# A trunk layer's output projection: from a plain product to a block product of seven, with the last branch computed in tile pairs

## The chip, the cores and the metric

The kernel runs on one core of a Trainium2 chip. Its engines work side by side, each through its own queue in order: TensorE (PE in the profile; the loading of its stationary operand is listed as PEld), VectorE (DVE), ScalarE (ACT), GpSimd (POOL) and SyncE (SP), which here only issues transfers. GpSimd issues transfers as well, those that add to what lies at the destination. The metric is the time of one execution on the device, in microseconds, as the median of several runs.

## The reference

Two layers (`DEPTH` = 2) over 512 tokens of width 1024. A layer projects its input, computes three branches (retention, chunked attention, differential attention), mixes them with sigmoid gates, and sends the mix through one output projection; a residual, a layer norm and a SwiGLU feed-forward part follow. The lines that matter:

```python
g = jax.nn.sigmoid(gates + b_merge[l]).reshape(B, S, N_BRANCHES, D)
merged = (g[:, :, 0] * jnp.einsum('bse,ed->bsd', o_a, w_branch_a[l])
          + g[:, :, 1] * jnp.einsum('bse,ed->bsd', o_b, w_branch_b[l])
          + g[:, :, 2] * jnp.einsum('bse,ed->bsd', o_c, w_branch_c[l]))
mix = jnp.einsum('bsd,de->bse', merged, w_out[l])
x = _layer_norm(DEEPNORM_ALPHA * x + mix, ln1_g[l], ln1_b[l])
```

`mix` is a product of 512 x 1024 with 1024 x 1024.

## The kernel before

**Precision.** Every float32 operand is carried as a pair, a high and a low part of 32 bits (`Pair`, with `hi` and `lo`); a product of two is three matmuls (`mm3`, L121 to L124): high by high, high by low, low by high. ScalarE makes the high part by a cast or an activation (L106 and L108 for activations, L154 and L271 for weights), VectorE the low part by a subtraction (L112, L114, L155, L272).

**Items.** The layer is a list of items, one after the other: an item is a block of weights (its `specs`) and a function that multiplies with it. `run_items` fetches the weights up to three items ahead (`AHEAD` = 3): a transfer into one of four staging tiles `st`, then the split into one of three buffers `wh` and `wl`. An item's split therefore waits until the matmuls of the item three before it are done. Small steps (the `s_...` functions) are handed to an item as groups and run between its halves (`between`). From this written order a scheduler makes the order of each engine's instructions; that order is fixed when the program is built, and each engine keeps to it on the chip.

**Block products.** The input projections and the feed-forward part already use the seven-product scheme (`Quarters`, `Halves`, `Chain`, `Close`, `Twins`). Activations and weights are cut into 2 x 2 blocks, and instead of eight block products there are seven, called m1, m2, y, x, v, g and h, of sums of blocks. `Quarters` holds the activation side for one pair of tiles k and k + 4 (features) with the two halves of the tokens as the other cut: m1, m2 and h are blocks as they are, `left` makes the sums for y and x (tile s12), `right` those for v and g (s43). For the weight side, `Chain` holds one staging tile: W11 for m1; to it GpSimd adds W12 (for y), then W22 (for x), then W21 (for h), each by a transfer that accumulates (`more`, L178). Such a transfer may begin only when the tile has been split for the product before it. A second tile, loaded ahead with `ahead_c`, holds the weights of g. m2 and v load theirs plainly. `product` computes 128 tokens of a block product in one bank of PSUM, 12 matmuls, twice per product; x, g and h go on accumulating on the banks of m1, and v on that of y, so a later product may not begin on a bank before VectorE has taken the earlier state from it.

**Around the change.** A gate block (`u_gate`, 256 columns) leaves two tiles `th`; those in `EARLY` are stored to DRAM and loaded again when a branch needs them. `u_branch` multiplies the branch by its weights (256 columns, four k-tiles for branch 2), applies the gate (L1080) and adds to the sum (L1084). After branch 2 it splits the sum of all eight tiles into pairs `mg`. The output projection is then three items: `u_out0` twice, for output columns 0 to 511 in four banks, and `u_out1`, columns 512 to 1023, token tile by token tile. `u_out1` adds the residual (`residual`, L1144), takes statistics, and normalises a token tile while PE works on the next (`Norm.normalise`, with one small power on GpSimd); transposes of finished tiles run between, and `to_T` makes the transposed, split input of the feed-forward part. The last of it, for the second half of the tokens, is `s_turned`, run inside the first feed-forward product.

## Time and profile before

| | us |
|---|---|
| median of 3 runs (1879.7 to 1881.35) | 1881.29 |
| the profiled execution | 1878.05 |
| its span, first to last instruction | 1876.3 |
| PE busy, 8802 matmuls | 1861.7 |
| VectorE busy | 1353.3 |
| ScalarE busy | 973.0 |
| GpSimd busy | 120.2 |

Times are from one profiled execution. A row of the timeline gives start, duration, engine, line of the kernel, operation and tiles, and in brackets the idle time before it and what ended that. A group's row gives a count, the busy time and the mean of one in ns. A wait's row says who waited for whom, the sum, how often, and the longest. Matmuls overlap, so what one costs is read from the distance of their starts. In the first layer the output projection runs from 553.6 (the first matmul into `pn`) to about 598.

### The profile page before, as it was taken

How to read it: one execution, taken by the hardware profiler on the slowest of the kernel's cores; microseconds unless marked ns; L12 is line 12 of the kernel's file. 1: busy time of each engine (PE TensorE's matmuls, PEld its weight loads, DVE VectorE, ACT ScalarE, POOL GpSimd, SP SyncE). 2: the span in 40 equal slices, each digit the busy share in tenths (PEclk: the TensorE clock that was granted, in tenths of full speed). 3: DMA queues.
4: the chain of work that ended last, by engine and by line, in shares of the span. 5: the costliest groups of instructions: out<-in, count | busy, mean ns of one | idle time of the engine just before them, and what ended most of it. 6: DMA issues, size and time to landing. Idle time of an engine off the chain costs nothing. (4 is left out here: it accounts for less than half of the span.)

```text
span 1876.3 us, 23317 instructions
## 1 busy us (share of the span) xinstructions
PE 1861.7 (99%) x8802; PEld 1553.8 (83%) x8802; DVE 1353.3 (72%) x2059; ACT 973.0 (52%) x1579; POOL 120.2 (6%) x145
## 2 busy tenths in 40 slices
PE   9999999999999999999999999999999999999998
PEld 7788888888888888888878888888888888888886
DVE  6777766667766776888686777566776667778886
ACT  5545555567643445554364546545666344455541
POOL 2000000000000000010020000000000001000100
PEclk9999999999999999999999999999999999999999
DMA  9585344332146577787386844533321547777871
GB/s 295 164 267 155 123 139 132 102 124 90 57 144 171 157 191 191 192 224 198 127 232 192 252 112 127 170 112 109 124 68 57 189 125 178 196 197 201 200 194 45
DMA packets 220320, 296.59 MB, mean 158 GB/s; under 512 B 8500, under 2 KB 115088, under 8 KB 220208
## 3 DMA queue, kind: packets, MB, share of 16 engines
q1 hardware_dynamic: 194096, 244.35, 39.3%
q0 software_dynamic: 26112, 50.76, 15.5%
q8 instruction: 69, 1.13, 0.2%
q14 instruction: 43, 0.35, 0.1%
HBM read 271.95 MB, written 23.12 MB: 157 GB/s over the span
## 5 line engine op out<-in xcount | busy, mean ns | idle before, releaser
L122 PE MATMUL pt<-xTh,wh 128*128 128x512 f32 x960 | 377.1, 393 | 2.1 <-ACT wh L154 2.0
L272 DVE TENSOR_TENSOR wl<-st,wh 128x2048 fp32r<-128x2048 f32 x126 | 288.1, 2289 | 119.3 <-ACT wh L271 118.7
L124 PE MATMUL pt<-xTh,wl 128*128 128x512 f32 x960 | 374.1, 390 | 0.0
L123 PE MATMUL pt<-xTl,wh 128*128 128x512 f32 x960 | 373.8, 389 | 0.0
L271 ACT CAST wh<-st 128x2048 fp32r<-128x2048 f32 x126 | 240.6, 1912 | 206.8 <-PE pf L124 107.8
L155 DVE TENSOR_TENSOR wl<-st,wh 128x1024 fp32r<-128x1024 f32 (+1 forms) x204 | 219.2, 1094 | 63.2 <-ACT wh L154 57.1
L154 ACT CAST wh<-st 128x1024 fp32r<-128x1024 f32 (+1 forms) x204 | 188.7, 949 | 115.4 <-PE pt L123 36.4
L122 PEld LDWEIGHTS pt<-xTh,wh 128*128 128x128 f32 x960 | 180.3, 188 | 39.3 <-ACT wh L154 2.9
L124 PEld LDWEIGHTS pt<-xTh,wl 128*128 128x128 f32 x960 | 180.2, 188 | 38.0
L123 PEld LDWEIGHTS pt<-xTl,wh 128*128 128x128 f32 x960 | 180.4, 188 | 36.2 <-DVE xTl L112 0.2
L122 PE MATMUL pf<-wh,xTh 128*128 128x512 f32 x336 | 132.6, 395 | 1.4 <-ACT rph L106 0.8
L123 PE MATMUL pf<-wl,xTh 128*128 128x512 f32 x336 | 131.1, 390 | 0.0
L124 PE MATMUL pf<-wh,xTl 128*128 128x512 f32 x336 | 131.0, 390 | 0.0
L746 ACT COPY tc<-pf 128x512 f32<-128x512 f32 x84 | 48.4, 588 | 80.5 <-PE pf L124 76.1
L122 PE MATMUL pf<-wh,s12h 128*128 128x512 f32 x224 | 88.0, 393 | 0.0
L122 PE MATMUL pf<-wh,s43h 128*128 128x512 f32 x224 | 87.3, 390 | 0.0
L123 PE MATMUL pf<-wl,s12h 128*128 128x512 f32 x224 | 87.3, 390 | 0.0
L124 PE MATMUL pf<-wh,s12l 128*128 128x512 f32 x224 | 87.2, 390 | 0.0
L123 PE MATMUL pf<-wl,s43h 128*128 128x512 f32 x224 | 87.2, 389 | 0.0
L124 PE MATMUL pf<-wh,s43l 128*128 128x512 f32 x224 | 87.2, 389 | 0.0
L122 PEld LDWEIGHTS pf<-wh,xTh 128*128 128x128 f32 x336 | 63.1, 188 | 16.5 <-ACT rph L106 1.6
L124 PEld LDWEIGHTS pf<-wh,xTl 128*128 128x128 f32 x336 | 63.0, 188 | 13.5 <-DVE xTl L112 0.4
(318 smaller groups left out, 3707.7 us busy)
## 6 DMA issues: line engine op xcount, KB each, us to landing
st<-in_w_in SPq DMA_DIRECT2D x61, 1024.0 KB, 5.1
st<-in_w_ffn_in SPq DMA_DIRECT2D x38, 1024.0 KB, 5.6
st<-in_w_ffn_in POOLq DMA_DIRECT2D x20, 1024.0 KB, 11.3
st<-in_w_ffn_out SPq DMA_DIRECT2D x20, 1024.0 KB, 7.8
st<-in_w_in SPq DMA_DIRECT2D x32, 512.0 KB, 5.0
st<-in_w_ffn_out POOLq DMA_DIRECT2D x16, 1024.0 KB, 9.2
st<-in_w_in POOLq DMA_DIRECT2D x12, 1024.0 KB, 10.6
th<-th SPq DMA_DIRECT2D x48, 256.0 KB, 4.3
```

What stands on the lines that cost most here:

```text
L122: nc.tensor.matmul(ps, lh, rh, start=start, stop=False, skip_group_check=onto)
L123: nc.tensor.matmul(ps, lh, rl, start=False, stop=False, skip_group_check=onto)
L124: nc.tensor.matmul(ps, ll, rh, start=False, stop=stop, skip_group_check=onto)
L154: return [nc.scalar.copy(self.hi[:, a:b], self.st[:, a:b]), nc.vector.tensor_sub(self.lo[:, a:b], self.st[:, a:b], f(self.hi[:, a:b]))]
L155: nc.vector.tensor_sub(self.lo[:, a:b], self.st[:, a:b], f(self.hi[:, a:b]))]
L271: nc.scalar.copy(self.hi, st)
L272: nc.vector.tensor_sub(self.lo, st, f(self.hi))
L746: nc.scalar.copy(t[to, j], ps)
```

## The change

The output projection becomes seven products of 24 matmuls (four k-tiles, two times 128 tokens, three matmuls each), with a `Chain` over `w_out`. `out_items` writes them in the order m1, m2, y, x, v, g, h; `plus` (now for both users) adds each product to the residual tiles z. The token tiles 0 and 1 are normalised after v, the tiles 2 and 3 after h; the transposes of the first half stand behind g, those of the second inside the first feed-forward product.

So that a pair of tiles is ready together, gate and branch blocks of branch 2 now compute the tiles i and i + 4 instead of 2i and 2i + 1, from two loads of 128 columns. The sum of the first is split at once for m1, that of the second for m2 and h; `left` and `right` follow as steps. Gate block 1 of branch 2 is no longer in `EARLY` and moves from before the differential attention to behind it; gate block 3 moves between the second and third block of branch 2. Some steps of the attention branches move to a neighbouring item.

```diff
-EARLY = [(0, 0), (0, 1), (0, 2), (0, 3), (2, 0), (2, 1)]
+EARLY = [(0, 0), (0, 1), (0, 2), (0, 3), (2, 0)]
...
+        def tiles(br, i):
+            return (i, i + 4) if br == 2 else (2 * i, 2 * i + 1)
+
+        def cols_of(w, c, br, i):
+            return [w[:, c + P * d:c + P * d + P] for d in tiles(br, i)] if br == 2 else [w[:, c + 256 * i:c + 256 * i + 256]]
...
-                    if br == 2:
-                        mg[d] = Pair("mg")
-                        split(mg[d], acc.pop(d), scale=0.5)
+                    if br == 2 and j == 0:
+                        q = mq[d] = Quarters()
+                        pr = HalfPair("m1")
+                        split(pr, acc[d][:, q.A], scale=0.5)
+                        q.put("m1", pr, q.A)
+                    elif br == 2:
+                        pr = Pair("m2")
+                        split(pr, acc[d], scale=0.5)
+                        mq[d - 4].put("m2", pr, q.A)
+                        mq[d - 4].put("h", pr, q.B)
...
-            (u_gate(1, 3), *d(6)), (u_branch(1, 3), *d(7)), (u_gate(2, 2), [s_d4(2)], [s_d2(3)]),
-            (u_gate(2, 3), [s_d3(3)], [s_d4(3)]),
-            (u_branch(2, 0),), (u_branch(2, 1),), (u_branch(2, 2),), (u_branch(2, 3),),
+            (u_gate(1, 3), *d(6)), (u_branch(1, 3), *d(7)), (u_gate(2, 1), [s_d4(2)], [s_d2(3)]),
+            (u_gate(2, 2), [s_d3(3)], [s_d4(3)]),
+            (u_branch(2, 0), [], [s_mleft(0)]), (u_branch(2, 1), [], [s_mleft(1)]), (u_gate(2, 3), [s_mright(0)], [s_mright(1)]),
+            (u_branch(2, 2), [], [s_mleft(2)]), (u_branch(2, 3), [], [s_mleft(3)]),
...
-        for i in range(2):
-            item(*u_out0(i, banks0))
-        item(rows_of(w_out[l], 512), u_out1)
...
+            hv = Chain(w_out[l], 0, 4)
...
+                    on = {"x": "m1", "g": "m1", "h": "m1", "v": "y"}.get(name, name)
+                    for j in range(2):
+                        t = 2 * i + j
+                        w[on, j] = product(mq, name, j, wt, w.pop((on, j), None))
+                        plus(x1, t, hf, w[on, j], op, last)
+                        if name in ("m2", "v", "h"):
+                            w.pop((on, j))
+                        if whole:
+                            x1["n"].normalise(t)
+                        between()
...
+        for (specs, fn), *groups in [
+            (o["m1"], [s_mright(2)], [o["c"]]), (o["m2"], [s_mright(3)]), (o["y"],), (o["x"],), (o["v"],),
+            (o["g"], [], [s_turned(0)]), (o["h"],),
+        ]:
+            item(specs, fn, *groups)
```

How the built programs stand at the places of the prediction, for the first layer. A number behind a name tells tiles of one name apart; in brackets stands what the instruction waits for (DMASW is a transfer issued by GpSimd, DMAHW one by SyncE).

ScalarE's queue before, at the start of the output projection: the weights of the last branch block and of the projection's items, and between them the high parts of the sums `mgh`.

```order
L154 CAST wh_4999<-st_4998 128x1024 [waits DMAHW6_49,PE_49,Activation_49]
L154 CAST wh_4999<-st_4998 128x1024
L154 CAST wh_5045<-st_5044 128x1024 [waits DMAHW0_49,PE_49,Activation_49]
L154 CAST wh_5045<-st_5044 128x1024
L108 ACTIVATE mgh_4948<-th_2583 128x512 [waits DVE_49]
L108 ACTIVATE mgh_4975<-th_2794 128x512
```

ScalarE's queue now: `wh_5079`, `wh_5150` and `wh_5256` are the weights of y, x and h, all from the chain's staging tile `st_4978`; `wh_5194` and `wh_5226` those of v and g; `m1_5050` is the fourth activation of m1, `s43h_5173` the fourth of v and g.

```order
L271 CAST wh_5079<-st_4978 128x2048 [waits DMASW4_49,PE_49,Activation_49]
L108 ACTIVATE s12h_5025<-sa_5022 128x512 [waits DVE_49]
L108 ACTIVATE m1_5050<-th_2584 128x256 [waits DVE_49]
L108 ACTIVATE m2h_5068<-th_3156 128x512 [waits DVE_49]
L108 ACTIVATE s12h_5075<-sa_5072 128x512 [waits DVE_49]
L271 CAST wh_5150<-st_4978 128x2048 [waits DMASW5_49,PE_49,Activation_49]
L271 CAST wh_5194<-st_5192 128x2048 [waits DMAHW0_49,PE_49,Activation_49]
L271 CAST wh_5226<-st_5147 128x2048 [waits DMASW3_49,PE_49,Activation_49]
L108 ACTIVATE s43h_5129<-sb_5126 128x512 [waits DVE_49]
L271 CAST wh_5256<-st_4978 128x2048 [waits DMASW6_49,PE_49,Activation_49]
L108 ACTIVATE s43h_5173<-sb_5170 128x512 [waits DVE_49]
```

Where the queue held casts of plain loads, three casts now wait for an accumulating transfer, and activations of m1 and of v stand behind them.

PE's queue now, in product v (banks `pf_5198` and `pf_5212`), from its seventh matmul on:

```order
L122 MATMUL pf_5198<-wh_5194,s43h_5129 128x512 [waits Activation_49]
L123 MATMUL pf_5198<-wl_5195,s43h_5129 128x512
L124 MATMUL pf_5198<-wh_5194,s43l_5130 128x512 [waits DVE_49]
L122 MATMUL pf_5212<-wh_5194,s43h_4940 128x512 [waits DVE_49]
L123 MATMUL pf_5212<-wl_5195,s43h_4940 128x512
L124 MATMUL pf_5212<-wh_5194,s43l_4941 128x512
L122 MATMUL pf_5198<-wh_5194,s43h_5173 128x512 [waits Activation_49]
```

PE's queue before, at the start of the projection: `mgh_4877` is the first of the eight sums, and the four banks take it in turn.

```order
L122 MATMUL pn_5088<-wh_4953,mgh_4877 128x512 [waits Activation_49]
L123 MATMUL pn_5088<-wl_4954,mgh_4877 128x512 [waits DVE_49]
L124 MATMUL pn_5088<-wh_4953,mgl_4878 128x512
L122 MATMUL pn_5089<-wh_4953,mgh_4877 128x512
L123 MATMUL pn_5089<-wl_4954,mgh_4877 128x512
```

The old projection multiplies sums that were split during the branch; the new one waits within a product for sums that are made while it runs. The same holds in m1, whose 14th matmul is the first to read `m1_5050`.

VectorE's queue before, between the two halves of the projection's output columns: `z` are the residual tiles, `pn` and `po` the banks.

```order
L1144 SCALAR_TENSOR_TENSOR z_5064<-z_5064,pn_5090 128x512 [waits DMAHW4_49,PE_49]
L1144 SCALAR_TENSOR_TENSOR z_5066<-z_5066,pn_5091 128x512 [waits DMAHW6_49,PE_49]
L478 BN_STATS bn_5086<-z_5064 128x6 [waits DVE_49]
L478 BN_STATS bn_5087<-z_5066 128x6 [waits DVE_49]
L272 TENSOR_TENSOR wl_5199<-st_5196,wh_5198 128x2048 [waits Activation_49]
L1144 SCALAR_TENSOR_TENSOR z_5061<-z_5061,po_5203 128x512 [waits DMAHW1_49,PE_49]
```

VectorE's queue now, from the last low part for v to the first addition of g, which frees a bank for h:

```order
L114 SCALAR_TENSOR_TENSOR s43l_5174<-sb_5170,s43h_5173 128x512 [waits Activation_49]
L1175 SCALAR_TENSOR_TENSOR z_5085<-z_5085,pf_5112 128x512 [waits DMAHW3_49,PE_49]
L1175 SCALAR_TENSOR_TENSOR z_5087<-z_5087,pf_5133 128x512 [waits DMAHW5_49,PE_49]
L272 TENSOR_TENSOR wl_5257<-st_4978,wh_5256 128x2048 [waits DMASW6_49]
L1177 TENSOR_TENSOR z_5085<-z_5085,pf_5198 128x512 [waits DVE_49,PE_49]
L1177 TENSOR_TENSOR z_5087<-z_5087,pf_5212 128x512 [waits DVE_49,PE_49]
L478 BN_STATS bn_5108<-z_5085 128x6 [waits DVE_49]
L478 BN_STATS bn_5109<-z_5087 128x6 [waits DVE_49]
L495 BN_AGGR mv_5274<-bn_5108 128x2 [waits DVE_49]
L272 TENSOR_TENSOR wl_5305<-st_5302,wh_5304 128x2048 [waits Activation_49]
```

Two weight blocks and the additions of x and v now stand between that low part and the addition that h waits for.

More of the change, by code (lines that the diff above doesn't have):

```diff
@@ L289, in put, with left @@
             self.use[name] = pr.hi[:, sl], pr.lo[:, sl]
-        def left(self, t1, t2):
+        def left(self, t1, t2, scale=None):
             a, b = self.A, self.B
@@ L1188, in layer, with plus, out_items, it @@
-        item(rows_of(w_out[l], 512), u_out1)
+                load_rows(x["z"][t], src[P * t:P * t + P])
+        def plus(x, t, hf, ps, op, final=False):
+            z = x["z"][t][hf]
+            if (t, hf) in x["fresh"]:
+                x["fresh"].remove((t, hf))
+                nc.vector.scalar_tensor_tensor(z, z, ALPHA, ps, op0=ALU.mult, op1=op)
+            else:
+                nc.vector.tensor_tensor(z, z, ps, op=op)
+            if final:
+                x["n"].stats(t, hf)
+        def out_items():
+            hv = Chain(w_out[l], 0, 4)
+            w = {}
+            def it(name, i, hf, op, last=False, whole=False):
+                def fn(wt):
+                    if name == "m1":
+                        load_res(x1, x_in if l == 0 else saved[2 * l - 1])
+                        x1["n"] = Norm(x1["z"], v["g1"], v["b1"], bcast_rows(ln1_g[l:l + 1]), bcast_rows(ln1_b[l:l + 1]),
+                                       x1T, saved[2 * l], x1f)
+                    on = {"x": "m1", "g": "m1", "h": "m1", "v": "y"}.get(name, name)
[8 more added lines that the diff above has]
+                        between()
+                return [getattr(hv, name)], fn
+            add, sub = ALU.add, ALU.subtract
+            return {"c": hv.ahead_c, "m1": it("m1", 0, 0, add), "m2": it("m2", 0, 0, add, True), "y": it("y", 1, 1, add),
+                    "x": it("x", 0, 1, sub), "v": it("v", 0, 1, add, True, True), "g": it("g", 1, 1, sub, True),
+                    "h": it("h", 1, 0, add, True, True)}
@@ L1329, in fn @@
                         for i, hf, op in adds:
-                            plus(2 * i + j, hf, w[on, j], op, gi == 1 and name == "h")
+                            plus(x2, 2 * i + j, hf, w[on, j], op, gi == 1 and name == "h")
                         if name in ("m2", "v", "h"):
@@ L1349, in plain @@
                     proj_N(hid, wts, t, ps, REST)
-                    plus(t, 0, ps, ALU.add, t < NT // 2)
+                    plus(x2, t, 0, ps, ALU.add, t < NT // 2)
                     between()
@@ L1359, in chase @@
                         n.transposes(t - 1)
-                    plus(t, 1, ps, ALU.add, True)
+                    plus(x2, t, 1, ps, ALU.add, True)
                     if last:
```

111 lines of the change are left out of this document (38 added, 73 removed).

## The prediction

> **What bounds the kernel now.** First the page: how much of the span TensorE (PE) works. Then the table of waits, for PE alone; then PE's timeline, because "busy" counts matmuls that overlap.
>
> ```profile
> span 1876.3 us, 23317 instructions
> PE 1861.7 (99%) x8802; PEld 1553.8 (83%) x8802; DVE 1353.3 (72%) x2059; ACT 973.0 (52%) x1579; POOL 120.2 (6%) x145
> ...
> core 0: 1876.3 us, clock 0.999
> ...
> PE pt L122 <- ACT wh L154: 2.0, 2, 1.3
> PE warm L583 <- POOL ident masks.py:199: 1.5, 1, 1.5
> PE pf L122 <- ACT rph L106: 0.8, 2, 0.4
> PE px L509 <- DVE z L500: 0.7, 2, 0.4
> ...
> 553.62 0.39 PE L122 MATMUL pn<-wh,mgh 128*128 128x512 f32 x1
> ...
> 555.88 0.39 PE L123 MATMUL pn<-wl,mgh 128*128 128x512 f32 x1
> ```
>
> PE waits for about 5 us in the whole span: every removed matmul is time won, every new wait is time lost. A 128x512 matmul is listed with 0.39 us, but ten start within 555.88 - 553.62 = 2.26 us, so one costs 0.226 us. That corrects the saving by almost half.
>
> **What is removed.** The projection had 8 x 8 x 3 = 192 matmuls in each layer; seven products of 24 are 168. 24 x 0.226 = 5.43 us a layer, 10.85 us in all. A product lasts 5.43 us; in this time whatever the next products need must be made. So the question is which of the new preparations take longer than their cover.
>
> **The chain of weight sums.** One staging tile holds W11 for m1, then by three GpSimd transfers the sums for y, x and h. Each can be issued only when VectorE has read the tile for the product before. The feed-forward part does the same with more work between; there one link is seen whole:
>
> ```profile
> 805.63 2.28 DVE L272 TENSOR_TENSOR wl<-st,wh 128x2048 fp32r<-128x2048 f32 x1
> ...
> 808.21 1.28 POOL L178 DMA_DIRECT2D st<-in_w_ffn_out  x1 [3.48 <-DVE wl L272]
> 824.82 1.28 POOL L178 DMA_DIRECT2D st<-in_w_ffn_out  x1 [15.33 <-DVE wl L272]
> ...
> 820.29 1.91 ACT L271 CAST wh<-st 128x2048 fp32r<-128x2048 f32 x1 [2.37 <-DMA st<-in_w_ffn_out]
> ...
> 822.23 2.29 DVE L272 TENSOR_TENSOR wl<-st,wh 128x2048 fp32r<-128x2048 f32 x1 [0.63 <-ACT wh L271]
> ...
> DMA to landing us min/median/max: 8.1/10.7/14.3
> ...
> DMA to landing us min/median/max: 8.3/10.1/12.0
> ```
>
> VectorE ends y's low half at 807.91, GpSimd issues at 808.21, the data lands 12.0 later (the last row is of the issues at 808.21 and 824.82: 12.0 and 8.3), ScalarE casts from 820.29, the low half is ready at 824.52: 16.6 us for a link. The row above it holds all 48 such transfers. In the new stage y is followed by x at once.
>
> When a link can start is set by the weight buffers: three, so an item's cast waits for the matmuls of the item three before.
>
> ```profile
> 564.74 2.00 ACT L154 CAST wh<-st 128x1024 fp32r<-128x1024 f32 x2 [6.06 <-PE pn L124]
> ...
> 596.40 1.92 ACT L271 CAST wh<-st 128x2048 fp32r<-128x2048 f32 x1 [0.58 <-PE po L124]
> ...
> 598.35 2.29 DVE L272 TENSOR_TENSOR wl<-st,wh 128x2048 fp32r<-128x2048 f32 x1 [1.18 <-ACT wh L271]
> ...
> 593.01 0.56 ACT L534 ACTIVATE xf<-px,colv 128x256 f32<-128x256 f32 x1 [15.47 <-PE px L509]
> 593.61 0.41 ACT L106 CAST xTh<-xf 128x256 fp32r<-128x256 f32 x1
> 593.92 0.56 ACT L534 ACTIVATE xf<-px,colv 128x256 f32<-128x256 f32 x1
> ...
> 574.82 1.28 DVE L478 BATCH_NORM_STATS2 bn<-z 128x6 f32<-128x512 f32 x2
> 576.02 1.27 DVE L1144 SCALAR_TENSOR_TENSOR z<-z,pn 128x512 f32<-128x512 f32 x2
> ...
> 612.99 1.42 DVE L112 TENSOR_TENSOR xTl<-xf,xTh 128x256 fp32r<-128x256 f32 x4
> ```
>
> The first cast began 0.3 us after the 48 matmuls that held its buffer (553.62 + 48 x 0.226 = 564.47). Cast and subtraction of a block take 600.64 - 596.40 = 4.24 us. Two 512-wide VectorE operations start 1.20 apart from the next two: 0.60 each; four 256-wide ones take 1.42: 0.35 each; a low half 2.2 back to back.
>
> Now in order, with 0 at m1's first matmul, in each layer:
> - m1's buffer is that of the last gate block, which ends 48 matmuls earlier, at -10.9. Low half ready at -10.9 + 0.3 + 4.24 = -6.3, the transfer W11+W12 issued at -6.0. Its landing is bounded by 8.1 and 14.3; little else moves then (one 1 MB load), so I take 8.5, by the 8.3 of the issue at 824.82: +2.5.
> - ScalarE's queue has y's cast ahead of the last s12 and of the high half of m1's fourth activation. The cast waits for the landing; then 1.92 + 0.55 + 0.35: 5.3. PE wants that activation with its 14th matmul, at 13 x 0.226 = 2.9. **Wait 2.4.** m1 ends at 5.3 + 11 x 0.226 = 7.8, m2 at 13.2, y at 18.7.
> - Behind s12 (4.95) VectorE has 0.6 + 0.35 + 0.6 and y's low half: 8.8. Issue 9.1. Now the eight loads of z and four of the norm's rows (3 MB) run beside it, so I take the median, 10.7: 19.8; x's low half at 24.0. x needs it with its second matmul at 18.9. **Wait 5.1**; x ends at 24.0 + 23 x 0.226 = 29.2.
> - Issue of h's sum at 24.3; the loads are over, 8.7: 33.0. ScalarE has h's cast ahead of the last s43 high half: 33.0 + 1.92 + 0.6 = 35.5. v wants it with its 13th matmul, at 29.2 + 2.7 = 31.9. **Wait 3.6**; v ends at 38.2, g at 43.6.
> - VectorE, held by that s43, then works off 0.6 + two additions for x 1.2 + h's low half 2.2 + two additions for v 1.2 + two statistics 1.2 + 0.2 + the next item's low half 2.2 + 0.5 + g's addition 0.6 = 9.9: 45.4. h accumulates on the bank that this addition reads. **Wait 1.8.** Two late steps of the normalisation stand right behind.
> - The first feed-forward product starts directly behind the transposes of the first half. A tile costs ScalarE 0.91 (593.01 to 593.92), with two half-block casts of about 1.0 between the first ones, while PE uses a tile in 6 x 0.226 = 1.36. Before, this half was ready a whole token tile earlier. Between 0 and 2.5, I take **1.1**, two gaps of about 0.55.
>
> Sum 2.4 + 5.1 + 3.6 + 1.8 + 1.1 = 14.0 lost against 5.4 won: +8.6 a layer, +17.1 us. With every landing at 8.1 and the last two terms zero, the waits are 2.0 + 2.5 + 3.0 = 7.5: +2.1 a layer. With landings 10.7, 14.3 and 10.7 they are 4.6, 8.8 and 5.6, and with 1.8 and 2.5 they make 23.3: +17.9 a layer.
>
> A page of the Trainium skill speaks against these terms. "DMA: Bandwidth & Descriptors", section "Anatomy of one DMA — SWDGE (gpsimd) path", fits a GpSimd transfer as 2.0 us plus bytes over 436 GB/s, an estimate of 4.4 us for 1 MB; by it nearly all of the waits vanish and the first rival is the result. The trace does not agree: 8.1 is its quickest of 48, and these transfers add to what is in the tile.
>
> **What I cost at nothing.** Gate and last branch in tile pairs are loaded as two transfers of 128 columns; the same gate and branch loads go away from one transfer of 256.
>
> ```profile
> st<-in_w_in SPq DMA_DIRECT2D x61, 1024.0 KB, 5.1
> ...
> st<-in_w_in SPq DMA_DIRECT2D x32, 512.0 KB, 5.0
> ...
> 480.00:500.00 20.00, 20.00 (x102) 16.97 (x101) 15.12 (x27) 15.42 (x28) 0.00 (x0) 1.00 0.09 27
> 500.00:520.00 20.00, 20.00 (x106) 17.01 (x105) 12.26 (x34) 9.80 (x28) 1.01 (x1) 1.00 0.24 79
> 520.00:540.00 20.00, 20.00 (x101) 16.80 (x100) 8.16 (x17) 6.84 (x18) 1.01 (x1) 1.00 0.40 131
> 553.00:575.00 22.00, 22.00 (x99) 18.22 (x98) 12.38 (x18) 6.73 (x9) 0.00 (x0) 1.00 0.81 261
> 575.00:597.00 22.00, 22.00 (x107) 18.40 (x106) 14.65 (x28) 5.23 (x8) 3.00 (x4) 1.00 0.39 74
> ```
>
> (Columns: stretch, length, then busy time of PE, PEld, DVE, ACT, POOL, clock, DMA share, GB/s.) The DMA engines are 9 to 40% busy from 480 to 540, where these loads run, and a load is issued items ahead; without that cover one costs its 5 us. One gate block no longer goes to DRAM and back: 4 stores and 4 loads of 256 KB less, hidden before too. Another moves from between the two attention branches to behind them; the first softmax of the differential attention then has 48 matmuls (10.9 us) of cover instead of 72. The last head has 48 now, without a PE wait in the table: nothing, or some 2 us a layer if VectorE (15 of 20 us from 480) is late. Three more weight blocks, six more additions and four left and right sums raise VectorE's work: it had 27 of 44 us in the old stage (the last two rows), and the rows from m1's first addition to the last normalisation now come to some 40 us beside 38 us of products. That makes VectorE no bound by itself, but leaves it no room to catch up after a wait; the 1.8 is the visible part.
>
> **Rivals.**
> 1. *The sums are hidden; faster.* x is on time if y's landing comes within 18.9 - 4.24 - 9.1 = 5.6 us in this reckoning, or 10.9 + 5.4 + 0.2 - 4.24 - 4.8 = 7.5 us if y's cast went out the moment its buffer is free; v would need 7.9 - 0.3 - 2.5 = 5.1. For it: in the feed-forward part such sums cost PE nothing. Against: there 16 us of other products stand between y and x, and no transfer took under 8.1. Time 1881.3 - 10.9 = 1870.
> 2. *The waits eat just the gain.* The quick ends of all landings, and VectorE catches up: 1881 to 1885.
> 3. *Slow restart.* If TensorE, after the waits at x and v, ran the rest of these products at half its pace, 23 + 12 matmuls cost 7.9 us more a layer: 1914. The rows show nothing on it, as PE never waits over 1.5 us and the clock is 0.999. The Trainium skill, "TensorE: Matmul & The Clock Gate", section "What's actually happening", has the clock halved after an idle window of about 3.4 us; no run here shows that so far.
>
> **How the numbers follow.** The profiled execution took 1878.05 us, 1.75 around its span; the sum gives 1895.2 on it. The median of the three runs is 3.24 higher, so 1881.29 + 17.1 = 1898. The chain with its waits, 1885 to 1917, has 0.72; rival 1 0.08; rival 2 0.06; rival 3 0.14, most of it below its full price. From 1885, the quick bounds, to 1916, near the slow ones, holds 8 in 10. Of one kernel, runs here differ by 0.1%, so 0.2% (3.8 us) is about what can be told from no change. Faster than 1877.5: rival 1 and a little, 0.09; within: most of rival 2, 0.07; slower 0.84.
>
> **What would show it.** PE's waits should list x's second matmul behind ScalarE and VectorE on the weights, with about 5 us, twice; m1's fourth activation with 2 to 3; v's last s43 with 3 to 4; h behind VectorE's addition. ScalarE's casts for y, x and h should be released by the staging tile's DMA. Matmuls of the stage should number 48 fewer, with the pitch still 0.226. It is wrong if the transfers land in under 7.5 us, if ScalarE's casts are not what stands in the way, or if waits appear in the attention part, where I have none.

## The result, and the profile after

| | before | after |
|---|---|---|
| median of 4 runs each, us | 1880.74 | 1924.55 (1921.61 to 1926.01) |
| ratio, with its 95% interval | | 1.0232 (1.0214 to 1.0249) |
| span of the profiled execution, us | 1876.3 | 1923.4 |
| matmuls | 8802 | 8754 |
| TensorE clock, mean granted | 0.999 | 0.990 |

The forecast was 1898, with a range from 1885 to 1916: the sign was right, the size was not. The page of the changed kernel, its table of waits (PE alone), and one row of its stretches:

```profile
span 1923.4 us, 23342 instructions
PE 1874.9 (97%) x8754; PEld 1553.5 (81%) x8754; DVE 1391.6 (72%) x2117; ACT 990.2 (51%) x1593; POOL 132.6 (7%) x153
...
PE pco L939 <- ACT cPh L106: 9.5, 2, 4.8
PE pf L122 <- ACT s43h L108: 6.4, 2, 4.8
PE psc L422 <- DVE cot L942: 5.4, 2, 2.7
PE pf L122 <- ACT m L108: 3.8, 2, 1.9
PE pf L123 <- DVE wl L272: 3.6, 2, 1.8
PE pf L122 <- ACT wh L271: 3.2, 2, 2.3
...
382.00:388.00 6.00, 5.28 (x15) 4.21 (x16) 1.75 (x4) 2.54 (x6) 1.04 (x2) 0.51 0.23 77
```

The 48 matmuls are gone. PE waits where it did not before, in two places: in the projection (`pf` behind `s43h`, `m`, `wl`, `wh`), and in the attention part (`pco`, `psc`). The forecast had nothing in the second place, where the waits of both layers come to 9.5 + 5.4 = 14.9 us. The last row is the stretch from about the end of the first `pco` wait on: 15 matmuls in 6 us, at a granted clock of 0.51.

Three matmuls divide a layer: the first of branch 0, the first of the projection, the first transpose into `ph` inside the feed-forward part. These rows of PE's timeline are before's (its projection's first matmul is in the prediction) and then after's, for the first layer:

```profile
270.60 0.39 PE L122 MATMUL pt<-oah,wh 128*128 128x512 f32 x1
...
685.63 1.03 PE L1232 MATMUL ph<-ident,tc 128*128 128x128 f32 x8
```

```profile
271.11 0.39 PE L122 MATMUL pt<-oah,wh 128*128 128x512 f32 x1
...
568.11 0.39 PE L122 MATMUL pf<-wh,m 128*128 128x512 f32 x1
...
711.54 1.03 PE L1265 MATMUL ph<-ident,tc 128*128 128x128 f32 x8
```

From the same rows in both layers, in us:

| stretch | before | after, layer 1 and 2 | difference, both layers |
|---|---|---|---|
| branch 0 to projection ("attention stretch") | 283.0, 283.0 | 297.0, 295.4 | +26.4 |
| projection to first `ph` ("projection stretch") | 132.0, 132.0 | 143.4, 140.8 | +20.1 |
| all the rest | | | +0.6 |

The projection came out near its forecast (+17.1). The attention stretch does the same matmuls in both kernels, and costs 26.4 us more. With that, 1898 becomes 1924.4. That this meets the measured median so closely is luck: the two spans differ by 47.1 us, the two medians by 43.8.

Where it comes from is in ScalarE's queue near 370 us. Before, with gate block (2,1) on PE, the casts of `ptr` come right behind the transposes, and `pco` starts on PE without a wait (last row):

```profile
370.86 0.69 ACT L1050 ACTIVATE th<-pt,hb 128x512 f32<-128x512 f32 x1
371.45 0.58 ACT L106 CAST cPh<-ptr 128x512 fp32r<-128x512 f32 x1
...
372.44 0.60 ACT L106 CAST cPh<-ptr 128x512 fp32r<-128x512 f32 x1
...
376.81 0.39 PE L939 MATMUL pco<-cPh,vhl 128*128 128x512 f32 x1
```

After, ScalarE's queue (first three rows), PE's (next four):

```profile
374.53 2.35 ACT L387 COPY sw<-pt 32x512 f32<-32x512 f32 x4
...
379.51 2.54 ACT L106 CAST ks<-rot 64x512 fp32r<-64x512 f32 x4 [1.98 <-DVE rot L391]
382.08 1.07 ACT L106 CAST cPh<-ptr 128x512 fp32r<-128x512 f32 x2
...
370.77 1.25 PE L452 MATMUL ptr<-ident,cE 128*128 128x128 f32 x10
...
382.72 0.80 PE L939 MATMUL pco<-cPh,vhl 128*128 128x512 f32 x1 [4.76 <-ACT cPh L106]
383.31 0.63 PE L122 MATMUL pt<-xTh,wh 128*128 128x512 f32 x1
383.74 0.63 PE L123 MATMUL pt<-xTl,wh 128*128 128x512 f32 x1
```

A gate block gives ScalarE one `tanh` a tile (0.69 us). The rotary block of head 0, which now carries these steps (`u_dqk(0)` with `c(7)`), gives it copies, and casts that wait for VectorE's rotation. They stand ahead of `cPh`: transposed at 370.77, cast at 382.08. So does the softmax of the next head (L439, 372.20 to 374.51), which was done before the transposes in the old order (366.97 to 369.26). PE waits 4.76 us, and afterwards 128x512 matmuls follow at 383.74 - 383.31 = 0.43 us instead of 0.227.

### The profile page after: what moved, and what is told of

Read it like the earlier page. It is cut to its first block, busy times and chain, and to the rows that moved or that the text cites. A ratio compares the mean times of both kernels' runs of the same rounds, so it can differ in the third digit from the quotient of the medians.

```text
span 1923.4 us, 23342 instructions
## 1 busy us (share of the span) xinstructions
PE 1874.9 (97%) x8754; PEld 1553.5 (81%) x8754; DVE 1391.6 (72%) x2117; ACT 990.2 (51%) x1593; POOL 132.6 (7%) x153
## 5 line engine op out<-in xcount | busy, mean ns | idle before, releaser
L272 DVE TENSOR_TENSOR wl<-st,wh 128x2048 fp32r<-128x2048 f32 x140 | 320.3, 2290 | 134.9 <-ACT wh L271 134.2
L271 ACT CAST wh<-st 128x2048 fp32r<-128x2048 f32 x140 | 267.3, 1914 | 249.6 <-PE pf L124 115.5
L155 DVE TENSOR_TENSOR wl<-st,wh 128x1024 fp32r<-128x1024 f32 (+1 forms) x188 | 200.8, 1085 | 69.1 <-ACT wh L154 46.8
L154 ACT CAST wh<-st 128x1024 fp32r<-128x1024 f32 (+1 forms) x188 | 173.5, 944 | 118.4 <-PE pt L123 44.5
L122 PE MATMUL pf<-wh,s43h 128*128 128x512 f32 x256 | 101.3, 396 | 6.4 <-ACT s43h L108 6.4
L122 PE MATMUL pf<-wh,s12h 128*128 128x512 f32 x256 | 101.5, 397 | 3.2 <-ACT wh L271 3.2
L123 PE MATMUL pf<-wl,s12h 128*128 128x512 f32 x256 | 101.0, 395 | 3.6 <-DVE wl L272 3.6
L123 PE MATMUL pf<-wl,s43h 128*128 128x512 f32 x256 | 100.9, 394 | 0.0
L124 PE MATMUL pf<-wh,s12l 128*128 128x512 f32 x256 | 100.7, 394 | 0.0
L124 PE MATMUL pf<-wh,s43l 128*128 128x512 f32 x256 | 100.3, 393 | 0.0
```

The source lines that it names most:

```text
L122: nc.tensor.matmul(ps, lh, rh, start=start, stop=False, skip_group_check=onto)
L123: nc.tensor.matmul(ps, lh, rl, start=False, stop=False, skip_group_check=onto)
L124: nc.tensor.matmul(ps, ll, rh, start=False, stop=stop, skip_group_check=onto)
L154: return [nc.scalar.copy(self.hi[:, a:b], self.st[:, a:b]), nc.vector.tensor_sub(self.lo[:, a:b], self.st[:, a:b], f(self.hi[:, a:b]))]
L155: nc.vector.tensor_sub(self.lo[:, a:b], self.st[:, a:b], f(self.hi[:, a:b]))]
L271: nc.scalar.copy(self.hi, st)
```

## The experiments

Stretches below are given as first layer, second layer, read from the same three matmuls. "Theory A" is that the moved gate block costs the attention stretch, "C" that the weight sums cost the projection stretch.

### The moved blocks undone, and done alone

`e1_attn_back`, the change with the old places of gate block (2,1) and (2,3):

```diff
-EARLY = [(0, 0), (0, 1), (0, 2), (0, 3), (2, 0)]
+EARLY = [(0, 0), (0, 1), (0, 2), (0, 3), (2, 0), (2, 1)]
...
-            (u_dqk(0), *c(7)), (u_gate(1, 0), *c(8)), (u_dqk(1), [v_back(dv)], [s_c3(7)] + d(0)[1]), (u_branch(1, 0), *d(1)),
...
+            (u_branch(0, 2), *c(4)), (u_cqk(3), *c(5)), (u_branch(0, 3), *c(6)), (u_gate(2, 1), *c(7)),
+            (u_dqk(0), *c(8)), (u_gate(1, 0), [v_back(dv)], [s_c3(7)] + d(0)[1]), (u_branch(1, 0), *d(1)), (u_dqk(1),),
...
-            (u_branch(2, 0), [], [s_mleft(0)]), (u_branch(2, 1), [], [s_mleft(1)]), (u_gate(2, 3), [s_mright(0)], [s_mright(1)]),
-            (u_branch(2, 2), [], [s_mleft(2)]), (u_branch(2, 3), [], [s_mleft(3)]),
...
+            (u_branch(2, 0), [], [s_mleft(0)]), (u_branch(2, 1), [s_mright(0)], [s_mleft(1)]),
+            (u_branch(2, 2), [s_mright(1)], [s_mleft(2)]), (u_branch(2, 3), [], [s_mleft(3)]),
```

> The changed kernel with the gate blocks of the last branch put back where they stood before: block (2,1) in the early list and under the end of the chunk attention, blocks (2,2) and (2,3) ahead of the four branch blocks, the rotary blocks back on their old steps. Tile pairs and the seven products stay; the steps that make the left and right sums move with the branch blocks. Theory A (the move of block (2,1) took the cover from the end of the chunk attention): branch a to projection goes from 297.0 and 295.4 us back to 283 to 285 in each layer, and the time from 1924.5 to about 1898 (1893 to 1905, since the sums now follow each other closer and the projection can lose a few us more). Rival B (tile pairs with their shorter packets, or the extra sums on ScalarE and VectorE, cost the 26 us): that stretch stays above 293 and the time above 1915.

Measured: attention stretch 283.0, 283.0; projection stretch 144.9, 144.7; 1904.91 us, ratio 1.0132 (1.0116 to 1.0147).

`e2_move_only`, the kernel before with the order of the change (the same lines the other way, old branch and projection items).

> The kernel before with only the order of the blocks of the change: block (2,1) out of the early list and behind the attention, block (2,3) between the branch blocks, the rotary blocks one step earlier; old tile columns, old projection. Theory A: branch a to projection becomes 295 to 297 us in each layer, and the time 1880.7 + 26.4 = 1907 (1902 to 1911), with the wait of the pco matmul for the cPh cast (4.8 us) in its profile. Rival B: 1881 within 2, the stretch at 283.

Measured: attention 296.2, 295.2; projection 132.0, 132.0; 1905.23 us, ratio 1.0138 (1.0122 to 1.0155). Its table of waits, PE alone:

```profile
PE pco L939 <- ACT cPh L106: 9.4, 2, 4.7
PE psc L422 <- DVE cot L942: 5.3, 2, 2.7
```

`e3_pairs_only`, the kernel before with `tiles` and `cols_of` of the change in `u_gate` and `u_branch`:

```diff
-                for j in range(2):
-                    d = 2 * i + j
+                for j, d in enumerate(tiles(br, i)):
...
-            return [([w[:, 256 * i:256 * i + 256]], nk)], fn
+            return [(cols_of(w, 0, br, i), nk)], fn
```

> The kernel before with only the tile pairs: the weights of the last branch and of its gate are fetched as two runs of 128 columns, tiles i and i+4 together; old order of blocks, old projection. Theory A: no price, 1881 within 2 us, branch a to projection 283. Rival B (shorter packets and twice the issues on SP delay the weights): 1888 or more, with waits of the pt matmuls for wh in the last branch.

Measured: 283.0, 283.0 and 132.0, 132.0; 1878.51 us, ratio 0.9995 (0.9985 to 1.0004). The two edits separate cleanly: the tile pairs and their split loads cost nothing, the move of the blocks (`e2`) costs 25 us, with the very waits of the change.

### Why the move costs that

The moved block could cost because PE has one block less over the same steps, or because the rotary block now stands where ScalarE's casts are wanted. Two runs exchange neighbours only, so the number of blocks stays.

`e14_swap_before`, the kernel before:

```diff
-            (u_branch(0, 2), *c(4)), (u_cqk(3), *c(5)), (u_branch(0, 3), *c(6)), (u_gate(2, 1), *c(7)),
-            (u_dqk(0), *c(8)), (u_gate(1, 0), [v_back(dv)], [s_c3(7)] + d(0)[1]), (u_branch(1, 0), *d(1)), (u_dqk(1),),
+            (u_branch(0, 2), *c(4)), (u_cqk(3), *c(5)), (u_branch(0, 3), *c(6)), (u_dqk(0), *c(7)),
+            (u_gate(2, 1), *c(8)), (u_gate(1, 0), [v_back(dv)], [s_c3(7)] + d(0)[1]), (u_branch(1, 0), *d(1)), (u_dqk(1),),
```

> The kernel before with only two neighbours exchanged: the rotary block of head 0 carries the steps c(7), and gate block (2,1) the steps c(8). As many blocks, as much TensorE work over the same steps. Theory H: the wait of pco for the cPh cast, 4 to 5 us, and some slow matmuls behind it appear, branch a to projection becomes 288 to 291 in each layer, the time about 1894 (1889 to 1898). Rival I: as the cover is the same, 283 to 284 and 1881 within 3 us.

Measured: attention 291.5, 290.4; 1894.59 us, ratio 1.0084 (1.0067 to 1.0101). Its table of waits has the one of `pco`, and none of `psc`:

```profile
PE pco L939 <- ACT cPh L106: 9.5, 2, 4.7
```

`e13_swap_after`, the changed kernel:

```diff
-            (u_dqk(0), *c(7)), (u_gate(1, 0), *c(8)), (u_dqk(1), [v_back(dv)], [s_c3(7)] + d(0)[1]), (u_branch(1, 0), *d(1)),
+            (u_gate(1, 0), *c(7)), (u_dqk(0), *c(8)), (u_dqk(1), [v_back(dv)], [s_c3(7)] + d(0)[1]), (u_branch(1, 0), *d(1)),
```

> The changed kernel with only two neighbours exchanged: gate block (1,0) carries the steps c(7) and the rotary block of head 0 the steps c(8), as a gate block and that rotary block did before the change; the rotary block of head 1 keeps the last steps of the chunk attention. Theory H (what costs is the rotary work of head 0 on ScalarE and VectorE under the steps c(7); the missing block itself costs little): the 4.8 us wait of pco for the cPh cast goes, with the slow matmuls behind it, branch a to projection falls from 297.0 and 295.4 us to 287 to 290, the time to about 1910 (1907 to 1914). Rival I (a block less of cover, wherever the rotary work stands): the wait only moves to the next step, the stretch stays at 294 or more and the time at 1920 or more.

Measured: attention 291.0, 290.7; 1915.11 us, ratio 1.0190 (1.0175 to 1.0205). The wait of `pco` is gone, but `psc` waits longer, 4.4 instead of 2.7 us:

```profile
PE psc L422 <- DVE cot L942: 8.8, 2, 4.4
```

Both theories hold a part. The rotary work under the steps `c(7)` is worth 8.5 and 7.4 us with as many blocks as before (`e14`); a gate block and a rotary block have 48 matmuls each. Taking it away from there gives back only 6.0 and 4.7, since the rotary block of head 1 still carries the last chunk steps and `psc` now waits for VectorE behind it. Theory H's 287 to 290 us and 1907 to 1914 us were each missed by about 1 us, and in `e14` its 288 to 291 by half a us in the first layer.

### The slow matmuls behind a wait

`e7_dummies`, the changed kernel with work for PE in the wait:

```diff
             def fn():
...
+                if h == 6:
+                    dum = bank("dum")
+                    for i in range(20):
+                        tc.keep_in_program_order(nc.tensor.matmul(dum, xT[0].hi[:, :P], xT[0].hi, start=i == 0, stop=i == 19))
                 ps = bank("pco")
```

> The changed kernel with 20 matmuls of 128x512 into a bank that nobody reads, put on TensorE right ahead of the first pco matmul that waited 4.8 us for the cPh cast, in each layer: 20 x 0.227 = 4.5 us of work in the place of the wait. Theory E (the wait makes the clock drop, and the 25 or so matmuls at 0.43 instead of 0.227 us behind it are a loss of their own): the wait goes to 0.2 to 0.5 us, the granted clock there stays at 1.00, the matmuls behind it come at 0.227, and the time falls by about 3 us a layer, to 1918 (1915 to 1921). Rival F (the slow matmuls have another cause, such as a slow operand or the accumulation of pco): they stay at 0.43 and the time at 1924 or more.

Measured: 1920.09 us, ratio 1.0213 (1.0199 to 1.0227). The same stretch as in the row of after above:

```profile
382.00:388.00 6.00, 5.40 (x25) 3.75 (x24) 3.22 (x6) 4.01 (x8) 1.04 (x2) 1.00 0.46 158
```

25 matmuls instead of 15, clock 1.00: with PE kept busy the slow stretch is gone, so it is a consequence of the wait, not of these operands. The attention stretch is 294.2 in the first layer (2.8 less, as expected) but 295.5 in the second, unchanged: there only 3.4 us behind `pco` had run at the half clock, and what ran so behind `psc` grew from 3.4 to 6.8 us. Of the 3.3 us between the two spans, 2.7 lie in the attention stretches; the projection stretches are 2.0 shorter, and the first branch block starts 1.4 later.

### The weight sums

`e4_plain_blocks` leaves out the sums of weight blocks: each product loads one block of `w_out` as it is. Its projection is therefore not the reference's.

```diff
-            hv = Chain(w_out[l], 0, 4)
+            hv = Plain(w_out[l], 0, 4)
...
+        def y(self):
+            return self.block(self.load(0, 1))
+        def x(self):
+            return self.block(self.load(1, 1))
```

> The changed kernel, with the sums of the weight blocks left out: each of the seven products loads one of the four blocks of the output projection's weight as it is, with a plain transfer on SP, so the projection computes something else; everything else stands as in the change. Theory C (the sums land 8 to 11 us after their issue, and casts for the next products stand behind them on the in-order ScalarE): the waits of the m1 product and of the x product go, the wait of the v product falls from 4.9 to under 2 us, projection to the first transposes of the FFN falls from 143.4 and 140.8 us to about 130 (128 to 134), and the time from 1924.5 to about 1900 (1895 to 1907). Rival D (the sums of the activations, not of the weights, hold the products: VectorE and ScalarE are full there): that stretch stays at 137 or more and the time at 1915 or more. The attention stretch is the same 297 and 295 in both.

Measured: projection stretch 128.8, 128.9; attention 294.7, 295.3; 1898.47 us, ratio 1.0100 (1.0085 to 1.0115). Theory C holds: all `pf` waits for `m`, `wh`, `wl` and `s43h` are gone, and the stretch is 2.2 us over the 132.0 - 5.4 = 126.6 that the saved matmuls leave. In the changed kernel the sums cost 14.6 and 11.9 us. ScalarE's queue in the changed kernel shows how:

```profile
570.29 1.90 ACT L271 CAST wh<-st 128x2048 fp32r<-128x2048 f32 x1 [4.85 <-DMA st<-in_w_out]
...
572.63 0.40 ACT L108 ACTIVATE m<-th 128x256 fp32r<-128x256 f32 x1
...
587.30 5.52 ACT L271 CAST wh<-st 128x2048 fp32r<-128x2048 f32 x3 [8.65 <-DMA st<-in_w_out]
...
602.10 1.90 ACT L271 CAST wh<-st 128x2048 fp32r<-128x2048 f32 x1 [6.43 <-DMA st<-in_w_out]
603.91 0.63 ACT L108 ACTIVATE s43h<-sb 128x512 fp32r<-128x512 f32 x1
```

It stands 4.85, 8.65 and 6.43 us before the casts of y, x and h, with `m` and `s43h` queued behind.

Three runs make the sums correctly in another way, in the order of the change. `e5_early_sums`: y's sum is accumulated ahead, the other two are VectorE additions, v comes ahead of x.

```diff
-            hv = Chain(w_out[l], 0, 4)
+            hv = Early(w_out[l], 0, 4)
...
-            (u_branch(2, 2), [], [s_mleft(2)]), (u_branch(2, 3), [], [s_mleft(3)]),
+            (u_branch(2, 2), [], [s_mleft(2)]), (u_branch(2, 3), [lambda: mo['a']()], [s_mleft(3)]),
...
-            (o["m1"], [s_mright(2)], [o["c"]]), (o["m2"], [s_mright(3)]), (o["y"],), (o["x"],), (o["v"],),
+            (mo["m1"], [s_mright(2)], [mo["c"]]), (mo["m2"], [s_mright(3)]), (mo["y"],), (mo["v"],), (mo["x"],),
```

> The changed kernel with the weight sums of the projection made another way: the sum for the y product is fetched and accumulated ahead, under the last branch block, the sums for x and h are two VectorE additions of 128x2048 (2.29 us each by the same additions of the kernel before), and v comes ahead of x; the attention stays as changed. Theory C (the chain of landings behind the in-order ScalarE): projection to the first transposes of the FFN falls from 143.4 and 140.8 us to about 131 (128 to 135), the time from 1924.5 to about 1902 (1896 to 1909). Rival D (VectorE and ScalarE are full there): the additions come on top and the stretch stays at 138 or more, the time at 1917 or more.

Measured: projection 134.3, 134.6; 1908.98 us, ratio 1.0156 (1.0142 to 1.0170). In its table of waits one is left in the projection, of x for its low part on VectorE, 4.5 us:

```profile
PE pf L123 <- DVE wl L272: 9.0, 2, 4.5
```

`e8_mixed`: x's sum goes back to GpSimd's transfer, behind the y product's casts.

```diff
+        def y(self):
+            b = self.block(self.a)
+            self.more(self.a, 1, 1)
+            return b
...
+        def x(self):
+            b = self.block(self.a)
+            self.e = self.load(1, 0)
+            nc.vector.tensor_add(self.e, self.e, self.__dict__.pop("a"))
+            return b
```

> The changed kernel with the sum for y accumulated ahead under the last branch block, the sum for x accumulated onto it by GpSimd behind the y product's casts with the v product now between y and x, and the sum for h by one VectorE addition; attention as changed. If what is left in the run with the two VectorE additions (134.3 us in that stretch, with a 4.5 us wait of the x product for its low part on VectorE) is VectorE's queue, that wait goes: projection to the first transposes 130 (128.5 to 132, the run with plain blocks had 128.8), the time about 1900 (1896 to 1904). Rival: the landing of x's sum, 10 us after its issue, is late again behind one product of 5.4 us, ScalarE waits for it, and the stretch is 134 or more, the time 1907 or more.

Measured: projection 142.6, 142.6; 1924.45 us, ratio 1.0239 (1.0225 to 1.0253). The rival holds, with a twist: VectorE has the addition for h early in its queue, and that waits for the same landing. VectorE's queue, then PE's waits:

```profile
588.47 2.29 DVE L276 TENSOR_TENSOR st<-st 128x2048 f32<-128x2048 f32 x1 [10.61 <-DMA st<-in_w_out]
...
PE pf L122 <- DVE z L1191: 15.1, 2, 7.7
```

10.61 us of standing on VectorE hold `z`'s additions, and PE 7.7 us behind them.

`e12_pool_sums`: the two additions of `e5` on GpSimd (`nc.gpsimd.tensor_add` for `nc.vector.tensor_add`).

> The run with early sums (1909 us, projection stretch 134.3 us, x waits 4.5 us for its low part on VectorE), with the two 128x2048 additions on GpSimd in the place of VectorE; attention as changed. No run shows how long GpSimd takes for such an addition. If VectorE's queue was what x waited for and GpSimd takes about as long as VectorE: the stretch falls to 130 (129 to 132), the time to about 1901 (1897 to 1905). Rival: GpSimd takes twice as long or more, x waits for it in place of VectorE, and the stretch stays at 134 or more, the time at 1908 or more.

Measured: projection 137.6, 137.8; 1917.13 us, ratio 1.0206 (1.0189 to 1.0223). The time is the rival's, but its cause is only half of it. An addition does take GpSimd twice VectorE's time (4.98 and 4.56 us against 2.29). What x waits for, 4.3 us, is still VectorE: its low part took 4.82 us in place of the 2.29 of the other blocks, in both layers, while GpSimd's second addition ran beside its first 2.7 us.

```profile
L268 POOL TENSOR_TENSOR st<-st 128x2048 f32<-128x2048 f32 x2 | 10.0, 4982 | 40.1 <-DMA z<-saved 21.0 <-DMA z<-in_x 19.1
...
582.61 4.56 POOL L274 TENSOR_TENSOR st<-st 128x2048 f32<-128x2048 f32 x1
...
584.51 4.82 DVE L286 TENSOR_TENSOR wl<-st,wh 128x2048 fp32r<-128x2048 f32 x1 [5.05 <-ACT wh L285]
...
PE pf L123 <- DVE wl L286: 8.7, 2, 4.3
```

That the one held up the other is what these rows suggest; no run separates it.

### Both causes removed at once

Four runs joined an undone move with other sums. `e11_plain_attn` is `e1` with the plain blocks of `e4` (the projection again not the reference's), `e6_early_attn` is `e1` with the sums of `e5`, `e10_mixed_attn` is `e1` with those of `e8`.

> The kernel with plain blocks in the place of the weight sums (so it computes something else, as there), and the gate blocks of the last branch back where they stood before the change. If the two causes add (A and C): branch a to projection 283, projection to the first transposes 129 (128 to 131), the time 1880.7 + 2 x (129 - 132) = about 1875 (1872 to 1880): faster than the kernel before by what the saved matmuls leave. Rival G (with no gate block between the branch blocks the sums of the activations come too late, whatever becomes of the weights): 136 or more in that stretch, waits of the pf matmuls for m2h, s12l or s43h, and the time 1889 or more.

> The sums made as in the run above, and the gate blocks of the last branch back where they stood before the change. If the two causes add (A and C): branch a to projection 283 in each layer, projection to the first transposes of the FFN 131 (128 to 134) against 132.0 before, and the time about 1879 (1873 to 1887), so about that of the kernel before. Rival: without block (2,3) between the branch blocks the left and right sums and the five casts come too close together, and the projection stretch is 136 or more, the time 1889 or more.

> The same sums, and all gate blocks of the last branch back where they stood before the change, so none between the branch blocks. The run with VectorE additions in this order had 150.9 us, with waits of 4.2 us (m2's cast on ScalarE) and 4.5 us (x's low part on VectorE). If the second was the queue of additions, the stretch falls to about 143 (139 to 147), and the time to about 1899 (1892 to 1907). Rival: both waits come from the casts and sums of the last branch that are too close, the stretch stays at 149 or more and the time at 1911 or more.

Measured, with attention 283.0 in all three: `e11` projection 141.5, 141.5, 1898.69 us, ratio 1.0105 (1.0090 to 1.0120); `e6` 150.9, 150.4, 1913.81 us, ratio 1.0180 (1.0166 to 1.0193); `e10` 153.8, 152.4, 1923.88 us, ratio 1.0234 (1.0220 to 1.0248). Each time the rival, and not the sum of two gains. Waits of PE in `e11`, where no weight sum is left:

```profile
PE pf L122 <- DVE z L1198: 4.1, 2, 2.1
PE pf L123 <- DVE wl L295: 2.9, 2, 1.5
PE pf L124 <- DVE s12l L114: 2.4, 2, 1.2
PE pf L122 <- DVE rs L520: 2.1, 2, 1.0
PE pf L122 <- ACT s43h L108: 1.9, 2, 0.9
PE pf L122 <- ACT m2h L108: 1.6, 2, 0.8
```

Many waits of 0.8 to 2.1 us, most on VectorE. The tiles that rival G named (`s12l`, `s43h`, `m2h`) account for 5.9 of the 15.0 us in these rows. The first layer's projection stretch, as a square:

| | weights by the chain | plain weights |
|---|---|---|
| block (2,3) between the branch blocks (as changed) | 143.4 | 128.8 |
| blocks where they stood before | 144.9 | 141.5 |

With plain weights the gate block between the branch blocks is worth 12.7 us a layer; by the waits above, it gives ScalarE and VectorE time for work that the projection needs, but no run takes that work apart. With the chain it is worth 1.5 us, and 3.9 in the second layer (144.7 against 140.8). The 12 to 14 us of the moved blocks in the attention stretch are paid either way.

`e9_mixed_shift` tried to have both blocks: `e8`, with (2,1) back under the chunk attention, (2,3) still between, and the missing place made on the rotary block of head 3:

```diff
-            (u_gate(1, 2), *d(4)), (u_branch(1, 2), *d(5)), (u_dqk(3),),
-            (u_gate(1, 3), *d(6)), (u_branch(1, 3), *d(7)), (u_gate(2, 1), [s_d4(2)], [s_d2(3)]),
-            (u_gate(2, 2), [s_d3(3)], [s_d4(3)]),
...
+            (u_gate(1, 2), *d(4)), (u_dqk(3), *d(5)), (u_branch(1, 2), *d(6)),
+            (u_gate(1, 3), *d(7)), (u_branch(1, 3), [s_d4(2)], [s_d2(3)]), (u_gate(2, 2), [s_d3(3)], [s_d4(3)]),
```

> The run above with block (2,1) back in the early list and under the end of the chunk attention, and block (2,3) still between the branch blocks: the place that is missing for the last attention steps is made by putting a group of steps of the second attention on the rotary block of head 3, so that all later groups come one block earlier. If the two costs are separate and this rotary block carries its group: branch a to projection 283 to 285, projection stretch 130, the time about 1876 (1872 to 1882), at or under the kernel before. Rival: steps on a rotary block cost there what they cost at head 0 (12 to 14 us a layer): branch a to projection 290 or more and the time 1890 or more.

Measured: attention 294.4, 293.8; projection 148.5, 150.6; 1935.11 us, ratio 1.0295 (1.0281 to 1.0309). The rival again; its waits of PE name the place, steps on a rotary block, and VectorE:

```profile
PE pf L124 <- DVE m L114: 18.4, 3, 9.3
PE ptr L468 <- DVE dE L1001: 16.9, 2, 8.5
```

No kernel tried is faster than the one before; `e3` equals it.

## Why the prediction was wrong in size, step by step

- **What is removed.** Right: 48 matmuls fewer, at 0.227 us where the clock is full. With plain weights the stretch came to 128.8 from 132.0.
- **The chain of weight sums.** The mechanism is shown (`e4`), the total close: 14.0 us lost a layer was forecast; 143.4 - 126.6 = 16.8 and 140.8 - 126.6 = 14.2 were lost. The closeness is in part luck: PE's waits in this chain came to 9.8 and 9.2 us, and most of the rest is half clock behind them, which the sum did not hold. The single terms shift. From GpSimd's issues of the sums (561.78, 577.12 and 591.83 in the first layer) to ScalarE's casts it took 8.5, 10.2 and 10.3 us; I had 8.5, 10.7 and 8.7. The waits, first and second layer: m1 1.9 and 1.9 (2.4 forecast); x 0.9 + 1.8 and 2.3 + 1.8 (5.1), less in the first layer because PE itself came 1.7 us late by the half clock behind m1; v 4.75 and 1.6 (3.6); h none and 1.05 (1.8); the first feed-forward product 0.5 and 0.4 (1.1).
- **What I cost at nothing.** This is the step that failed. I wrote of the moved gate block "nothing, or some 2 us a layer". It costs 13.2 and 12.2 us alone (`e2`) and 14.0 and 12.4 in the change. I had looked at the differential attention's first softmax and counted its cover in matmuls. The wait arose in the chunk attention, one block earlier, and for some 8 of the 13 us not from missing matmuls (in `e14` none are missing) but from what the block that moved up brings to ScalarE and VectorE, ahead of casts that PE needs. The loads in pairs did cost nothing (`e3`).
- **Rivals.** The first, that the sums are hidden, fell: no landing under 8 us in these rows. The second, that the waits just eat the gain, fell with the time. The third, the slow restart at a chance of 0.14, took place, but as an addition to the waits, and as much of it behind `pco` and `psc`, which I had not forecast, as in the projection. The mean granted clock fell from 0.999 to 0.990: 0.009 x 1923 = 17 us of pace not granted, at most, because part of it fell into idle time. I gave it 7.9 a layer in the projection as a way of its own instead of a term behind each wait; in the first projection it was worth at most 1.7 + 3.4 = 5.1 us, by the rows at the end. The rule of the Trainium skill ("TensorE: Matmul & The Clock Gate", "What's actually happening") agrees with the trace in the halving; on what triggers it, see below.
- **What would show it.** The last sentence named the failure: it is wrong "if waits appear in the attention part, where I have none". They did.

## What to carry to other kernels

When a change moves a block of work, price what comes into its old place: list, for each in-order engine, what the block that moves up issues, and see who stands behind it; cover counted in TensorE work alone says nothing of that. An instruction that waits for a slow transfer blocks its engine for all behind it, whichever engine is chosen (ScalarE in the change, VectorE in `e8`), so sums that arrive late need a place in the queue that is late too. And a wait of TensorE here often costs more than its length: where it left about half or more of a window of 3.4 us idle (next section), matmuls at half pace followed.

## What the runs showed of the hardware

The granted clock is not lowered by degrees. Stretches of the changed kernel (columns as in the prediction), behind m1's wait and behind v's:

```profile
573.00:574.00 1.00, 0.92 (x3) 0.72 (x4) 1.00 (x3) 0.03 (x1) 0.00 (x0) 0.63 1.01 371
574.00:575.00 1.00, 1.00 (x4) 0.81 (x3) 1.00 (x2) 0.58 (x1) 0.00 (x0) 0.50 1.04 391
575.00:576.00 1.00, 1.00 (x4) 0.81 (x3) 1.00 (x1) 0.05 (x1) 0.00 (x0) 0.50 1.06 391
576.00:577.00 1.00, 1.00 (x4) 0.76 (x4) 1.00 (x2) 0.00 (x0) 0.00 (x0) 0.67 1.06 397
...
588.00:590.00 2.00, 0.88 (x3) 0.19 (x1) 0.76 (x1) 2.00 (x2) 0.00 (x0) 1.00 0.00 0
590.00:592.00 2.00, 0.41 (x2) 0.37 (x3) 2.00 (x2) 2.00 (x2) 0.17 (x1) 1.00 0.00 0
...
604.00:606.00 2.00, 1.41 (x3) 1.17 (x4) 1.43 (x3) 0.53 (x2) 0.00 (x0) 0.50 1.03 260
606.00:608.00 2.00, 2.00 (x6) 1.58 (x5) 2.00 (x2) 0.00 (x0) 0.00 (x0) 0.50 0.04 11
608.00:610.00 2.00, 2.00 (x6) 1.52 (x6) 1.25 (x2) 0.00 (x0) 0.00 (x0) 0.50 0.06 13
610.00:612.00 2.00, 2.00 (x9) 1.60 (x8) 1.89 (x4) 1.84 (x1) 0.00 (x0) 0.80 0.91 261
```

It is 0.50 or 1.00 and mixtures of both in time. Behind the wait of 1.9 us in m1 it loses 0.37 + 0.5 + 0.5 + 0.33 = 1.7 us of clock, so it was low for 3.4 us; behind v's 4.75 us it loses 3 x 1.0 + 0.4 = 3.4, so 6.8 us, twice that. Yet x's waits, 2.7 us with a matmul between them near 588 to 592, did not lower it, and neither did m1's wait in the second layer, 1.92 us. The length of the wait alone does not decide.

The trace also records when the clock changes: in the first layer at 382.11, 388.94, 416.24, 419.66, 573.25, 576.67, 603.98 and 610.80 us. The distances (6.83, 27.30, 3.42, 153.59, 3.42, 27.31, 6.82) are all whole multiples of 3.413 us to within rounding. The second layer continues the same grid, and every other trace here in which the clock changes has such a grid of its own. So one can cut the time into these windows and ask how long PE stood idle in each (the length of the window less PE's busy time in it), in the changed kernel:

| window starts at | PE idle in it, us | clock in the next window |
|---|---|---|
| 378.70 (wait of `pco`) | 3.41 | 0.50 |
| 412.83 (wait of `psc`) | 1.85 | 0.50 |
| 569.84 (m1, first layer) | 1.87 | 0.50 |
| 586.91 (x, first layer) | 1.44 | 1.00 |
| 590.32 (x, first layer) | 1.27 | 1.00 |
| 600.56 (v, first layer) | 3.42 | 0.50 |
| 1525.57 (m1, second layer) | 1.39 | 1.00 |
| 1542.64 (x, second layer) | 2.31 | 0.50 |

From the full clock, 1.85 us or more of idle time in one window brought the half clock in the next, 1.44 or less did not: m1's wait lies inside one window in the first layer and is split between two in the second. Over all traces here the border is near half a window: 1.79 us and more lowered the clock, up to 1.75 did not, with one exception at 1.51. A low window was followed by a second one where PE still stood idle for 0.61 us in it (from 382.11 and from 603.98), and not where it worked throughout (from 573.25); hence 6.8 us and 3.4. This agrees with the account in the Trainium skill ("TensorE: Matmul & The Clock Gate", "What's actually happening") of windows of about 3.4 us that run freely. It does not agree with a wholly idle window as the condition: about half a window was enough. No run set the idle time on purpose, so the exact border stays open.

A 128x2048 float32 addition took GpSimd 4.98 and 4.56 us, in the run with the sums there (`e12`), against 2.29 on VectorE; a VectorE subtraction of that size that ran beside one took 4.82.
